# The last 256-column product of row 0 goes from VectorE to a ScalarE copy and a GpSimd multiply

## The chip, the cores and the metric

The kernel runs on one core of one Trainium2 chip. The metric is the device time of one execution in microseconds (us). The kernel before takes 296.96 us as the median of three runs (296.96 to 297.09).

The engines are named as the profile names them. PE is TensorE's matmul, PEld its weight load, DVE is VectorE, ACT is ScalarE, POOL is GpSimd, SP is SyncE. A name with a q behind it (POOLq, SPq, ACTq) is the queue of that engine, where semaphore waits, branches, drains and the issue of transfers appear. PSUM is held in eight banks of 128 x 512 float32.

## The reference

```python
batch, m, k, n = 16, 512, 1024, 768
x:  (batch, m, k) float32      w1, w2: (k, n) float32

y1 = np.matmul(x, w1)
y2 = np.matmul(x, w2)
return (np.tanh(y1) * y2).astype(np.float32)
```

Seen as a matrix, x has 8192 rows of 1024, which are 64 row blocks of 128. Each of the two products has 768 columns.

## The kernel before, in words

**Tiling.** The matrices are cast to float16. The columns of both weights are put into three blocks of 512: block a is the first 512 columns of w1, block b the first 512 columns of w2, and block g holds the last 256 columns of w1 and the last 256 columns of w2 side by side. For each row block the output needs the tanh of a times b (512 columns) and the tanh of the left half of g times its right half (256 columns).

**Head.** The first four row blocks (`HEAD`) are computed plainly, 8 matmuls for each of the three blocks, while the weights are still arriving. Their x is brought in on SP, cast by DVE (`cx..`), transposed on PE (`PT..`), and copied out of PSUM by `evacuate` (`e..`) on ACT or DVE. The part of the fourth row block that needs block b is done at the very end as filler (`m3y0..` and `m3y1..`, 8 short matmuls each, then the multiplies `mub3X` and `mub3Y`).

**Triples.** The other 60 row blocks come in 20 triples. A triple (three row blocks, two halves of the 1024, three column blocks) would need 18 products of 4 matmuls each. A bilinear scheme makes it 15 products, `p0` to `p14`, of sums of x blocks (`S..`, on DVE) with sums of weight blocks (`B..`, on DVE, once). The results are put together in PSUM by copies and seeds on ACT (`copy..`, `seed..`) and by additions on DVE (`add..`), as the list `C_OPS` says. Then follow the tanh on ACT (`t0`..`t2` for 512 columns, `th0`..`th2` for 256) and the multiply on DVE (`m0`..`m2` for 512, `mh0`..`mh2` for 256), and the rows are stored from SP, at the end also from ACT.

**A check beside it.** Absolute sums of every x row block (`D..`, 1024 columns on ACT, written to a scratch tile called `junk`) and of the weights (`aw..`) are compared with limits; five small steps (`flag_1` to `flag_5`) make one flag `bad`. After the last step of the plan every engine loads `bad` (L817) and branches (L818, `tc.If`) around `general_path`, which isn't run here. After that comes the end of the program (put down to L911): each engine drains, and they meet at a barrier. In program order these instructions stand behind everything that the plan has put on the same engine.

**The order of the work.** The class `Planner` (L75) makes it before the program is built. Each step is an `op` with a name, its cost on each engine that may do it, a due time and its needs; the planner plays the steps through with these costs, takes for each engine the step that can start first (or is due first), gives out the PSUM banks and returns one list. Every instruction is then pinned in that order (`pin`). So a changed cost can change the order on all engines and the number of the banks, and a step with one engine in its costs is always on that engine. The order of the 15 products on PE is strict (`plan.strict`), as three strings give it (`PE_ORDER`, `FIRST_ORDER`, `LAST_ORDER`).

**Around the change.** Before the plan's list, `constants` (L335) runs the seven matmuls of `WARM` (L250) on a constant tile while nothing has arrived yet; each goes to a PSUM bank of its own. `by_pe` (L587) gives the costs of the transposes and of the copies `e..` behind them: 0.5 on ACT for the first four row blocks and for the next three. POOL has the loads of x with a cast (L362), of block b (L359), and 18 tiny copies that hold the loads back (L501); after the last load at L362 the plan gives it nothing.

At the end, the last five steps on DVE are `add4`, `m1`, `mh1`, `mh0` (all of the last triple) and `mub3Y`; the last ones on ACT are `th1` and `th0`. The last four stores are `st620` (row block 62, columns 0 to 511) on ACT, `st621` (row block 62, columns 512 to 767) on SP, `st611` (row block 61, the 256 columns that `mh0` makes) on ACT, and `st3Y` on SP.

Of the kernel before, what the change touches and what calls it, by code (L numbers as in the profile page):

```python
# [9 lines left out]
ALU = mybir.AluOpType  # L10
# [64 lines left out]
class Planner:  # L75
# [9 lines left out]
    def op(self, name, engines, due, needs, fn, *args, behind=(), issued=(), chains=(), xfer=0.0, latency=None, seeds=False,  # L85
           lands=None, hold=0.0):
        assert name not in self.ops, name
        self.ops[name] = dict(engines=engines, due=due, needs=[n for n in needs if n], behind=[n for n in behind if n], issued=[n for n in issued if n], fn=fn, args=args,
                              chains=chains, xfer=xfer, latency=latency, seeds=seeds, lands=lands, hold=hold)
        for c in chains:  # L90
            self.chains.setdefault(c, {"left": 0, "bank": None, "end": 0.0, "act": 0.0, "dve": 0.0})["left"] += 1
# [135 lines left out]
def kernel(  # L227
# [7 lines left out]
    nc = tc.nc  # L235
# [6 lines left out]
    F = 512  # L242
    G = N - F
    HEAD = 4
    TRIPLES = (MT - HEAD) // 3
# [1 line left out]
    FP32 = ((0, 0), (1, 0))  # L247
    LOW, HIGH = 512.0, 1024.0
    XT_BUFS, XH_BUFS, S_BUFS, O_BUFS, C_BUFS = 12, 8, 2, 9, 2
    WARM = 512, 512, 512, 512, 512, 512, 512  # L250
    FILL = 512, 512, 256
    FREE = 3
    TURNS = (2, 0, 1), (0, 2, 1)
# [6 lines left out]
    bf16, f16, f32, i32 = mybir.dt.bfloat16, mybir.dt.float16, mybir.dt.float32, mybir.dt.int32  # L260
# [17 lines left out]
    junk = once.tile([P, K], f16, name="junk")  # L278
# [29 lines left out]
    pin = tc.keep_in_program_order  # L308
    engine = {"dve": nc.vector, "act": nc.scalar, "pool": nc.gpsimd, "sp": nc.sync}
    plan = Planner(8)  # L310
    op = plan.op

    def bank(chain):
        return banks[plan.chains[chain]["bank"]]
# [108 lines left out]
    def out_tile(mt):  # L423
        return o_bufs[mt if mt < HEAD else HEAD + (mt - HEAD) % O_BUFS]
# [21 lines left out]
    def place(i, name):  # L446
        if name[0] == "c":
            return bank((i, name))
        return c_bufs[name, i % C_BUFS]

    def slot_casts(name):
        n = S_NAMES.index(name) * C_BUFS
        return [f"c{s}{k}" for j, (s, k) in enumerate(slices) if s != "b" and n <= j % SLOTS < n + C_BUFS] + [f"cx{HEAD + 2}0"] * (n <= STAGED < n + C_BUFS)
# [19 lines left out]
    def c_mul(e, i, r, src, lo, n, at):  # L473
        o = out_tile(HEAD + 3 * i + r)[:, lo:lo + n]
        pin(nc.vector.tensor_tensor(o, o, place(i, src)[:, at:at + n], ALU.mult))  # L475

    def c_aside(e, r, src, borrowed):
        pin(nc.scalar.copy(out_tile(borrowed)[:, :F], place(0, src)))

# [77 lines left out]
    for n, what in enumerate(by_pool):  # L557
        if what in GATES:
            after, src = GATES[what]
            op(f"gate{what}", {"pool": 0.1}, 0.1 * n, [after], gate, src, issued=issued)  # L560
            issued = [f"gate{what}"]
        if what[0] == "b":
            name = f"c{what}"
            op(name, {"pool": 0.58}, 0.1 * n, [], load_w, "b", int(what[1]), issued=issued, lands=lands[what])
        else:
            mt, h = int(what[1]), what[2:]
            free = [f"cx{m}{k}" for m in range(2, HEAD) for k in range(2) if xh_place(m) == xh_place(mt)]
            name = f"L{mt}{'abc'[int(h)] if h else ''}"
# [18 lines left out]
    def by_pe(mt, h, due, load):  # L587
        fp32 = (mt, h) in FP32
        op(f"PT{mt}{h}", {"pe": 0.44 if fp32 else 0.24}, due, [load], transpose_pe, mt, h, ("T", mt, h), chains=[("T", mt, h)])
        op(f"e{mt}{h}", {"dve": 0.6 if fp32 else 0.45, "act": 0.5} if mt < HEAD else {"act": 0.5}, due + 0.4, [f"PT{mt}{h}"], evacuate, mt, h, ("T", mt, h),  # L590
           chains=[("T", mt, h)])

    for n, after in enumerate(("PT00", "PT10")):
# [25 lines left out]
    outs = {mt: [] for mt in range(MT)}  # L619

    def reuse_out(mt):
        aside = [f"{name}.0" for name, (borrowed, _) in ASIDE.items() if mt == borrowed]
        return aside + [f"st{mt - O_BUFS}"] if mt >= HEAD + O_BUFS else []
# [16 lines left out]
    for n, s in enumerate("agb"):  # L640
        for mt in range(HEAD):
            if (s, mt) == ("b", HEAD - 1):
                continue
            due, behind = (lambda n: landed[slices["agb".index(s) * KO + n]] + 0.8 + 0.02 * mt), []
            finals(mt, s, due(KO - 1) + (5.0, 3.0, 7.0)["agb".index(s)], plain(mt, s, due, behind))

    mt = HEAD - 1
# [31 lines left out]
    def w_needs(v, ks=slice(0, KH)):  # L679
        if v in wsum:  # L680
            return [f"B{v}.{p.start}" for p in parts(v) if p.start < ks.stop and ks.start < p.stop]
        bit = v.bit_length() - 1
        return [f"c{s}{bit // 3 * KH + k}" for s in "abg"[bit % 3] for k in range(ks.start, ks.stop)]
# [5 lines left out]
    def x_needs(i, v):  # L689
        if v & (v - 1):  # L690
            return [f"S{v}.{i}"]
        bit = v.bit_length() - 1
        mt = HEAD + 3 * i + bit // 2
        return [f"e{mt}{bit % 2}"] if mt < BY_PE else [f"T{mt}"]
# [7 lines left out]
    def needed(i, v):  # L702
        return min([slot_of[i, o[0]] for o in C_OPS if o[1] == "p" and o[4] == v] + [needed(i, u) - 0.5 for u, a, b, _ in A_SUMS if v in (a, b)])

    for i in range(TRIPLES):
        for name, kind, needs, *_ in C_OPS:
            soonest[i, name] = max([until[i, n] for n in needs] + ([slot_of[i, name]] if kind == "p" else []))
            until[i, name] = soonest[i, name] + TIME[kind] + 0.2
        for v, a, b, how in A_SUMS:
            op(f"S{v}.{i}", {"dve": 0.335}, None, x_needs(i, a) + x_needs(i, b), x_sum, i, v, a, b, how,  # L710
               hold=needed(i, v) - S_AHEAD if i > 1 else 0.0,
               behind=[f"{r}.{i - S_BUFS}" for r in a_readers[v]] if i >= S_BUFS else first_done)
            for u in (a, b):
                if not u & (u - 1):
                    xt_readers[HEAD + 3 * i + (u.bit_length() - 1) // 2].append(f"S{v}.{i}")
        for o in C_OPS:
            name, kind, needs = o[:3]
            needs = [f"{n}.{i}" for n in needs]
            chains = sorted({(i, p) for p in o[3:6] if isinstance(p, str) and p[0] == "c"})
            if kind == "p":  # L720
                needs += x_needs(i, o[4]) + w_needs(o[5])
                op(f"{name}.{i}", {"pe": SLOT}, slot_of[i, name], needs, product, i, *o[3:], chains=chains,
                   behind=[f"m{HEAD - 1}y0{KO - 1}"] if (name, i) == ("p3", TRIPLES - 1) else [])
                if not o[4] & (o[4] - 1):
                    xt_readers[HEAD + 3 * i + (o[4].bit_length() - 1) // 2].append(f"{name}.{i}")
                continue
            if kind in ("seed", "copy", "add"):
                before = []
                if o[3][0] == "s":
                    before = [f"{r}.{i - C_BUFS}" for r in readers[o[3]]] if i >= C_BUFS else slot_casts(o[3])  # L730
                if kind == "add":
                    op(f"{name}.{i}", {"dve": 0.6}, None, needs, c_add, i, *o[3:], behind=before, chains=chains, seeds=True)
                else:
                    op(f"{name}.{i}", {"act": 0.495}, None, needs, c_copy, i, *o[3:], behind=before, chains=chains, seeds=True)
                continue
            r = o[3]
            mt = HEAD + 3 * i + r
            due = soonest[i, name] + LAST
            if kind in ("t", "th"):
                lo, n = (0, F) if kind == "t" else (F, G)  # L740
                op(f"{name}.{i}", {"act": 0.5 if n == F else 0.285}, due, needs, c_tanh, i, r, o[4], lo, n, o[5],
                   behind=reuse_out(mt) + ([f"{FIRST_READER[name]}.{i}"] if i == TRIPLES - 1 and name in FIRST_READER else []), chains=chains)
            elif i == 0 and name in ASIDE:
                borrowed, at = ASIDE[name]
                op(f"y{name}.0", {"act": 0.5}, due + 1, [n for n in needs if n[0] != "t"], c_aside, r, o[4], borrowed, chains=chains)
                op(f"{name}.0", {"dve": 0.6}, at + 6, [f"y{name}.0"] + [n for n in needs if n[0] == "t"], aside_mul, r, borrowed, hold=at)
                outs[mt].insert(0, f"{name}.0")
            elif kind == "m" and i < HALVED:
                for t in range(2):
                    op(f"{name}{'xy'[t]}.{i}", {"dve": 0.335}, due + 1, needs, c_mul, i, r, o[4], t * G, G, t * G, chains=chains)  # L750
                    outs[mt].append(f"{name}{'xy'[t]}.{i}")
            else:
                lo, n, at = (0, F, 0) if kind == "m" else (F, G, G)
                op(f"{name}.{i}", {"dve": 0.6 if n == F else 0.335}, due + 1, needs, c_mul, i, r, o[4], lo, n, at, chains=chains)
                outs[mt].insert(0 if kind == "m" else 1, f"{name}.{i}")
    for mt in range(MT):
        i = (mt - HEAD) // 3 if mt >= HEAD else -1
# [29 lines left out]
    for mt in range(HEAD, MT):  # L787
        i, r = divmod(mt - HEAD, 3)
        r = turn[mt] - HEAD - 3 * i
# [13 lines left out]
    pin(nc.vector.memset(ones, 2.0 ** -12))  # L803
    for n, cols in enumerate(WARM):
        constants(banks[n], cols)
    for n in sorted(soon, key=lambda n: plan.start_of[n]):
        o = plan.ops[n]
# [3 lines left out]
    for n in order:  # L811
        if n not in soon:
            o = plan.ops[n]
# [102 lines left out]
```

## Time and profile before

| | |
|---|---|
| median of three runs | 296.96 us |
| the profiled execution | 297.16 us |
| its span, from the first to the last instruction | 295.6 us (1.56 us less) |
| mean granted TensorE clock | 1.000 |
| PE busy | 289.5 us, 98% of the span, 1374 matmuls |
| DVE busy | 255.8 us, 87%, 552 instructions |
| ACT busy | 224.4 us, 76%, 454 instructions |
| POOL busy | 42.3 us, 14%, 94 instructions |

Times in the views are counted from the start of the span. A row of the timeline has the start, the length, the engine, the line, the operation, what it writes and reads, how many instructions it merges, and in brackets the idle time before them with what ended it. In a view of one line, three numbers with strokes are the shortest, median and longest duration in ns, then follow the start of the first and of the last in us. Instructions of the queues (POOLq and so on) aren't counted as busy.

### The profile page before, as it was taken

To read this page: it belongs to the slowest core of one execution; us is meant where nothing else is said; L and a number is where in the kernel's file an instruction comes from. 1 tells how busy PE (TensorE), PEld (TensorE's weight loads), DVE (VectorE), ACT (ScalarE), POOL (GpSimd) and SP (SyncE) were. 2 spreads that over 40 slices of the span, in tenths; PEclk is the share of its full clock that TensorE was granted. 3 is DMA by queue.
4 is the path that set the end of the run, shared out by engine and by line. 5 is a ranking of instruction groups with operands and counts; after the bars stand their busy time and mean duration, and the time that the engine had idled before them with its cause. 6 is when DMAs were issued, how large, how long until landed. Compare 5 with 4: busy or idle time off the path is not lost. (4 is left out here: it accounts for less than half of the span.)

```text
span 295.6 us, 4588 instructions
## 1 busy us (share of the span) xinstructions
PE 289.5 (98%) x1374; PEld 132.3 (45%) x1374; DVE 255.8 (87%) x552; ACT 224.4 (76%) x454; POOL 42.3 (14%) x94
## 2 busy tenths in 40 slices
PE   7999999999999999999999999999999999999994
PEld 3445444444444444444444444444444444444442
DVE  1679999999989998898989888898988889898875
ACT  2698599799878878877888888677777767778442
POOL 0065022202102102202012021020211100000000
PEclk9999999999999999999999999999999999999999
DMA  6999999999999999989999999999999999241234
GB/s 217 391 321 204 182 141 169 210 247 230 240 194 197 247 226 216 252 218 239 204 190 246 231 236 270 164 271 264 224 298 225 213 175 324 104 162 53 109 136 169
DMA packets 84858, 63.63 MB, mean 215 GB/s; under 512 B 62816, under 2 KB 67168, under 8 KB 84832
## 3 DMA queue, kind: packets, MB, share of 16 engines
q1 hardware_dynamic: 73888, 45.10, 59.7%
q0 software_dynamic: 9936, 16.65, 36.0%
q10 hardware_dynamic: 1008, 1.57, 1.5%
q8 instruction: 11, 0.18, 0.2%
q14 instruction: 15, 0.12, 0.1%
HBM read 39.85 MB, written 25.17 MB: 220 GB/s over the span
## 5 line engine op out<-in xcount | busy, mean ns | idle before, releaser
L457 PE MATMUL bank<-b,early_x 128*128 128x512 f16 x640 | 148.3, 379 | 0.0
L457 PEld LDWEIGHTS <-early_x 128*128 128x128 f16 x800 | 78.1, 98 | 94.3 <-DVE early_x L421 0.3
L467 DVE TENSOR_TENSOR bank<-bank,arena 128x512 f32<-128x512 f32 x100 | 69.6, 696 | 13.6 <-ACT arena L461 10.9
L461 ACT ACTIVATE arena<-bank 128x512 f32<-128x512 f32 x100 | 57.6, 596 | 18.1 <-PE bank L457 18.1
L475 DVE TENSOR_TENSOR o<-o,bank 128x256 f32<-128x256 f32 (+1 forms) x128 | 61.9, 516 | 7.3 <-ACT o L470 5.9
L390 ACT ACTIVATE junk<-xh 128x1024 f16<-128x1024 f16 x60 | 63.4, 1057 | 0.1
L457 PEld LDWEIGHTS <-xT 128*128 128x128 f16 x400 | 39.0, 98 | 46.9 <-issue 0.4
L457 PE MATMUL bank<-b,xT 128*128 128x512 f16 x240 | 58.3, 379 | 0.0
L470 ACT ACTIVATE o<-bank 128x256 f32<-128x256 f32 (+1 forms) x80 | 34.8, 438 | 26.0 <-DVE bank L467 22.8
L457 PE MATMUL bank<-wh,xT 128*128 128x512 f16 x160 | 41.0, 379 | 0.0
L457 PE MATMUL bank<-wh,early_x 128*128 128x512 f16 x160 | 40.9, 379 | 0.0
L362 POOL DMA_DIRECT2D xh<-in_x_dram x61 | 32.4, 540 | 16.6 <-ACT junk L390 8.6
L421 DVE TENSOR_TENSOR early_x<-early_x,xT 128x512 f16<-128x512 f16 x80 | 33.5, 420 | 0.5
L470 ACT ACTIVATE o<-arena 128x512 f32<-128x512 f32 x40 | 25.2, 629 | 7.5 <-DVE arena L467 7.5
L501 POOL CAST held<-xT 128x1 f32<-128x1 f16 x18 | 4.5, 251 | 161.3 <-DMA xT<-xh 161.3
L461 ACT ACTIVATE bank<-bank 128x512 f32<-128x512 f32 x40 | 21.4, 570 | 4.7 <-PE bank L457 3.9
L430 PE MATMUL bank<-wh,xT 128*128 128x512 f16 x72 | 19.5, 379 | 0.3
L467 DVE TENSOR_TENSOR arena<-bank,arena 128x512 f32<-128x512 f32 x20 | 13.7, 686 | 3.6 <-ACT arena L461 3.6
L421 DVE TENSOR_TENSOR early_x<-xT,xT 128x512 f16<-128x512 f16 x40 | 16.7, 418 | 0.0
L421 DVE TENSOR_TENSOR early_x<-xT,early_x 128x512 f16<-128x512 f16 x40 | 16.7, 418 | 0.0
L467 DVE TENSOR_TENSOR bank<-arena,bank 128x512 f32<-128x512 f32 x20 | 13.8, 692 | 0.1
L390 ACT ACTIVATE junk<-wh 128x768 f16<-128x768 f16 x16 | 13.6, 847 | 0.1
(51 smaller groups left out, 140.0 us busy)
## 6 DMA issues: line engine op xcount, KB each, us to landing
out_dram<-o SPq DMA_DIRECT2D x59, 384.0 KB, 5.1
xh<-in_x_dram POOLq DMA_DIRECT2D x58, 256.0 KB, 6.7
arena<-in_w_dram SPq DMA_DIRECT2D x12, 256.0 KB, 5.6
early_x<-in_x_dram SPq DMA_DIRECT2D x8, 256.0 KB, 4.9
arena<-in_w_dram ACTq DMA_DIRECT2D x4, 256.0 KB, 5.9
wh<-in_w_dram POOLq DMA_DIRECT2D x8, 128.0 KB, 5.5
xT<-xh SPq DMA_TRANSPOSE x57, 4.2
out_dram<-o SPq DMA_DIRECT2D x3, 256.0 KB, 2.5
```

Of the source, the lines that this page charges most:

```text
L362: pin(nc.gpsimd.dma_start(xh(mt)[:, cols], xf[mt][:, cols]))
L390: pin(nc.scalar.activation(junk[:, :src.shape[-1]], src, ACT.Abs, scale=scale, accum_out=sums[:, column:column + 1]))
L421: pin(engine[e].tensor_tensor(x_operand(i, v), x_operand(i, a), x_operand(i, b), OP[how]))
L430: pin(nc.tensor.matmul(bank(chain)[:, :rhs.shape[-1]], xt(mt)[:, k, :], rhs, start=first, stop=k == KO - 1, skip_group_check=True))
L457: pin(nc.tensor.matmul(place(i, dst), x_operand(i, a)[:, k, :], w_rhs(b, k), start=begins and k == 0, stop=k == KH - 1, skip_group_check=T ...
L461: pin(nc.scalar.activation(place(i, dst), place(i, src), ACT.Copy, scale=float(sign)))
L467: pin(nc.vector.tensor_tensor(place(i, dst), a, b, ALU.add if signs == (1, 1) else ALU.subtract))
L470: pin(nc.scalar.activation(out_tile(HEAD + 3 * i + r)[:, lo:lo + n], place(i, src)[:, :n], ACT.Tanh, scale=float(sign)))
L475: pin(nc.vector.tensor_tensor(o, o, place(i, src)[:, at:at + n], ALU.mult))
L501: pin(nc.gpsimd.tensor_copy(held, xt(mt)[:, 0, :1]))
```

## The change

Three things are changed. `WARM` has its last matmul of 512 columns cut into two of 256, the second of which goes to the eighth bank. The planner's cost of a copy `e..` on ACT is 0.59 in place of 0.5 for the first four row blocks. And in the last triple `mh0` isn't done by DVE out of PSUM: a new step `ymh0` lets ACT copy the 256 columns from PSUM to the scratch tile `junk`, and `mh0` multiplies them into the output tile on POOL. It can only be on POOL, at a cost of 0.7 in the plan.

The order that follows from it: on DVE the last steps are `add4`, `m1`, `mh1`, `mub3Y`. On ACT `ymh0` stands behind `th0`, ahead of the stores. The last stores are `st620` and `st3Y` on SP, `st621` and `st611` on ACT. On POOL the multiply stands behind the last load of x and ahead of POOL's load of `bad` and its branch. In the head, the copy `e31` goes from DVE to ACT, the abs pass `D1` moves from before the first weight casts to behind them, `D2` and `D3` each move one place back (`D3` now stands between `e61` and `e40`), and `p10` of the first triple comes ahead of `PT51`. Some steps of ACT and DVE in the first four triples change places, and on SP the store `st4` comes ahead of the transpose `T16`. From there to the end the order on every engine is the same as before, with other bank numbers.

```diff
-    WARM = 512, 512, 512, 512, 512, 512, 512
+    WARM = 512, 512, 512, 512, 512, 512, 256, 256
...
+    def c_spare(e, i, src, at):
+        pin(nc.scalar.copy(junk.bitcast(f32)[:, :G], place(i, src)[:, at:at + G]))
+
+    def spare_mul(e, r):
+        o = out_tile(HEAD + 3 * (TRIPLES - 1) + r)[:, F:F + G]
+        pin(nc.gpsimd.tensor_tensor(o, o, junk.bitcast(f32)[:, :G], ALU.mult))
...
-        op(f"e{mt}{h}", {"dve": 0.6 if fp32 else 0.45, "act": 0.5} if mt < HEAD else {"act": 0.5}, ...
+        op(f"e{mt}{h}", {"dve": 0.6 if fp32 else 0.45, "act": 0.59} if mt < HEAD else {"act": 0.5}, ...
...
+            elif (name, i) == ("mh0", TRIPLES - 1):
+                op("ymh0", {"act": 0.29}, due + 0.3, needs[:1], c_spare, i, o[4], G, chains=chains)
+                op(f"{name}.{i}", {"pool": 0.7}, due + 1, ["ymh0"] + needs[1:], spare_mul, r)
+                outs[mt].insert(1, f"{name}.{i}")
```

More of the change, by code (lines that the diff above doesn't have):

```diff
@@ L589, in by_pe @@
         op(f"PT{mt}{h}", {"pe": 0.44 if fp32 else 0.24}, due, [load], transpose_pe, mt, h, ("T", mt, h), chains=[("T", mt, h)])
-        op(f"e{mt}{h}", {"dve": 0.6 if fp32 else 0.45, "act": 0.5} if mt < HEAD else {"act": 0.5}, due + 0.4, [f"PT{mt}{h}"], evacuate, mt, h, ("T", mt, h),
+        op(f"e{mt}{h}", {"dve": 0.6 if fp32 else 0.45, "act": 0.59} if mt < HEAD else {"act": 0.5}, due + 0.4, [f"PT{mt}{h}"], evacuate, mt, h, ("T", mt, h),
            chains=[("T", mt, h)])
```

## The prediction

> **What bounds the kernel now.** I read the busy times by stage first, from 60 us on and then the end.
>
> ```profile
> core 0: us, PE busy (x) PEld busy (x) DVE busy (x) ACT busy (x) POOL busy (x), PEclk, DMA share, GB/s
> 60.00:100.00 40.00, 40.00 (x187) 18.11 (x186) 37.65 (x87) 35.12 (x74) 5.36 (x12) 1.00 1.12 224
> 250.00:280.00 30.00, 30.00 (x142) 13.62 (x140) 25.74 (x58) 21.21 (x42) 0.00 (x0) 1.00 0.31 122
> 290.00:295.60 5.60, 1.33 (x11) 0.78 (x8) 2.04 (x5) 0.66 (x2) 0.00 (x0) 1.00 0.59 209
> ```
>
> PE is busy in all of both middle stages, at a granted clock of 1.00. The change takes no matmul away, so the middle cannot get shorter; it could only get longer if PE were made to wait. What is left to gain or lose lies in the head and in the last stage, where PE has 1.33 us of work in 5.6. The groups of PE by shape show how little PE idles:
>
> ```profile
> L457 PE MATMUL bank<-b,early_x 128*128 128x512 f16 x640 | 148.3, 379 | 0.0
> L430 PE MATMUL bank<-wh,xT 128*128 128x512 f16 x72 | 19.5, 379 | 0.3
> L337 PE MATMUL bank<-ones 128*128 128x512 bf16 x11 | 4.4, 538 | 1.3 <-DVE ones L803 1.3
> ```
>
> The end is read from the timeline, DVE, ACT and the two queues that store:
>
> ```profile
> 289.66 0.69 DVE L467 TENSOR_TENSOR bank<-arena,bank 128x512 f32<-128x512 f32 x1
> 290.29 1.04 PE L430 MATMUL bank<-wh,xT_kept 128*128 128x256 f16 x8
> 290.39 0.66 ACT L470 ACTIVATE o<-bank 128x256 f32<-128x256 f32 x2 [1.06 <-DVE bank L467]
> 290.55 1.35 DVE L475 TENSOR_TENSOR o<-o,bank 128x512 f32<-128x512 f32 x3 [0.19 <-issue]
> 291.27 1.17 ACTq L427 DMA_DIRECT2D out_dram<-o  x2
> 291.81 0.41 DVE L437 TENSOR_TENSOR o<-o,bank 128x256 f32<-128x256 f32 x1
> 292.26 0.33 SPq L427 DMA_DIRECT2D out_dram<-o  x1
> ```
>
> The DVE row of three is `m1`, `mh1`, `mh0`; the row at 291.81 is `mub3Y`, which ends at 292.22. SP then issues the last store at 292.26. The queue of SP waits for it, and the program ends after a barrier:
>
> ```profile
> SPq L911 <- DMA out_dram<-o: 0.8, 3, 0.3
> L911 SPq DRAIN  x3: 7/7/130, 294.7 to 295.3; - x3
> L911 POOLq EVENT_SEMAPHORE  x4: 17/17/17, 294.7 to 295.5; - x4
> ```
>
> SP's first drain stands at 294.7, when the stores have landed. POOL's first wait at the barrier is met at 294.7 too, and 0.9 us later the span is over. So today the last store sets the end, and POOL is ready early. How early, and with what, is the row on which this prediction rests. POOL's queue, from its load of `bad` on (lines 817, 818 and 911):
>
> ```profile
> L817 POOLq TENSOR_LOAD <-bad x1: 496/496/496, 274.3 to 274.3; - x1
> L818 POOLq COMPARE_BRANCH  x2: 38/42/45, 274.9 to 276.8; - x2
> L818 POOLq INC_SWDGE_SEM  x1: 1576/1576/1576, 275.2 to 275.2; - x1
> L911 POOLq DRAIN  x3: 45/107/5758, 277.2 to 295.3; - x3
> L911 POOLq DRAIN  x2: 45/76/107, 294.9 to 295.3; - x2
> ```
>
> The last line is the same view from 290 us on: the two late drains took 45 and 107 ns, so the one of 5758 ns is the one that began at 277.2. From the load of `bad` at 274.3 POOL needs 0.5 for the load, 1.6 for the semaphore step, a branch, and 5.76 for the drain, until 277.2 + 5.76 = 283.0: 8.6 us. Today nobody sees them, since they are over 11.7 us before the barrier.
>
> **The change part by part.**
>
> *The copy of 256 columns on ACT.* `th1` and `th0` are the ACT row at 290.39: two in 0.66, each 0.38, so the second starts 0.28 behind the first and ends at 291.05. `ymh0` reads the same bank and follows at the same step: start 290.95, and at the 0.38 of a 256-column ACT row it ends at 291.33. ACT's stores begin at 291.27 only, so the copy delays the first one of ACT at most to 291.33, and that one is now `st621`, which needs `mh1` (the DVE row of three ends at 291.90, and `mh1` one step of 0.33 before, at 291.57). Cost on the path: nothing.
>
> *DVE without `mh0`.* `mub3Y` moves up by one step of 0.33 (from 291.81 to 291.48; PE's last matmul has ended by 290.29 + 1.04 = 291.33). Its store on SP moves to 291.93.
>
> *The multiply on POOL.* The trace has no two-input operation on POOL. The nearest rows:
>
> ```profile
> 1.26 0.29 POOL masks.py:199 TENSOR_SCALAR_AFFINE_SELECT ident<-ident 128x128 f32<-128x128 f32 x1
> L475 DVE TENSOR_TENSOR o<-o,bank 128x256 f32<-128x256 f32 x80 | 31.9, 416 | 5.2 <-ACT o L470 5.2
> 17.68 0.44 POOL L504 CAST held<-wh 128x1 f32<-128x1 f16 x1 [16.13 <-DVE wh L368]
> 17.18 0.43 DVE L368 CAST wh<-arena 128x512 f16<-128x512 f32 x1 [0.78 <-DMA arena<-in_w_dram]
> ```
>
> Twice the 0.29 of 128 columns is 0.58; twice DVE's own 0.42 is 0.83. Lower end 0.42, upper end four times DVE, 1.7; I take 0.7, near the POOL row with room for the second input. The start: the cast at 17.68 began 0.07 after the DVE row it waited for ended (17.61). So the multiply runs from 291.40 to 292.10, and `st611` can be issued on ACT at 292.13, against 292.26 for the last issue today. By the data alone, then, the end comes 0.13 us earlier; with the multiply at 0.83 it is even, at 1.7 it is 0.9 later, and at 0.42 the bound is `st3Y`, 0.33 earlier. In a sentence beside it: the Trainium skill, GPSIMD Engine Reference, section 3.1, gives about 2.6 cycles of 1.2 GHz for an element of such an operation, an estimate of 0.55 us for 256 and a dispatch on top; the sum by it stays the same within 0.1.
>
> *What is queued behind the multiply.* This decides. Until now POOL went from its last load of x straight to its load of `bad`, at 274.3. Now the multiply stands ahead of it, and POOL's sequencer gets past it only when ACT's copy is done, at 291.40. DVE's row shows that a sequencer then runs on while its engine works:
>
> ```profile
> L817 DVEq TENSOR_LOAD <-bad x1: 539/539/539, 291.4 to 291.4; - x1
> ```
>
> (291.4, before DVE's last multiply starts at 291.81.) So POOL loads `bad` at 291.4 and not at 274.3, and the same 8.6 us of load, semaphore step, branch and drain end at 300.0. If the load has to wait for the multiply to be done (292.1), it is 300.7. The barrier, met at 294.7 so far, is met at 300.0 to 300.7; the 0.9 behind it stays. I take 300.0, because of the DVE row. The stores have landed by 294.6 and no longer matter. The span grows by 300.0 - 294.7 = 5.3.
>
> For the drain: bounds are 0 (it waited for something that would be over by then) and 5.76. I take 5.76. Nothing on POOL was running but its own semaphore step, its last transfer had been issued at 236.8, and its waits of line 911 begin at 294.7 only:
>
> ```profile
> 236.81 0.53 POOL L362 DMA_DIRECT2D xh<-in_x_dram  x1 [2.87 <-ACT junk L390]
> ```
>
> The Trainium skill, Perfetto Trace Analysis, section "Sequencer-only Instruction (DRAIN, etc)", says that such a row holds execution only and not the wait for a semaphore; with that, the 5.76 would be POOL's own work.
>
> *The copies at 0.59 in the plan.* They change the head's order. PE up to `PT01` is as before. Then two places matter. `e31` on ACT ends as early as on DVE, and the g block's first matmul waits for the weight cast at 17.18 + 0.43 in any case. And `D3` now runs between `e61` and `e40`:
>
> ```profile
> 25.10 1.05 ACT L390 ACTIVATE junk<-early_x 128x1024 f16<-128x1024 f32 x1
> 26.55 0.59 ACT L366 COPY xT<-bank 128x512 f16<-128x512 f16 x1 [0.31 <-PE bank L380]
> 27.68 1.07 ACT L366 COPY xT<-bank 128x512 f16<-128x512 f16 x2 [0.54 <-PE bank L380]
> 28.79 0.43 DVE L421 TENSOR_TENSOR early_x<-xT 128x512 f16<-128x512 f16 x1
> 31.40 1.89 PE L457 MATMUL bank<-b,early_x 128*128 128x512 f16 x8
> ```
>
> `e61` starts at 26.55, the next step on ACT 0.49 later, `D3` takes 1.05, so `e40` starts at 28.1 in place of 27.68 and ends at 28.7, just when PE, with `p10` moved ahead, comes to `PT51`, which goes into the same bank. The first sum `S3` needs `e41` and starts at 29.2 in place of 28.79; but `add64` (0.6) now comes after `S15`, so `S15`, for which `p6` (at 31.40) waits, ends at about 31.0 in place of 31.3. PE loses nothing here; bounds -0.1 and +0.4, and I take 0. The moved steps of the first triples have the slack of the row 60 to 100, where DVE idles 2.3 us of 40 and PE does not: 0.
>
> *The warm-up cut in two.* One more weight load and matmul while PE waits:
>
> ```profile
> 1.30 3.17 PE L337 MATMUL bank<-ones 128*128 128x512 bf16 x7 [1.30 <-DVE ones L803]
> 4.67 0.44 PE L380 MATMUL bank<-ident,early_x 128*128 128x128 f32 x1 [0.21 <-DMA early_x<-in_x_dram]
> ```
>
> The seven end at 4.47 and the first transpose waits for x until 4.67: hidden; 0.15 at most.
>
> **The sum.** Span 295.6 + 5.3 = 300.9; outside the span there are 1.56, so 302.5 for the profiled execution, which was 0.20 above the median. Predicted for the median: 302.3 us.
>
> **The rivals.**
>
> *The drain is short when it comes late.* For it: at the start a drain of POOL took 184 ns, and behind a semaphore step of 27 ns:
>
> ```profile
> L900 POOLq INC_SWDGE_SEM  x1: 27/27/27, 0.1 to 0.1; - x1
> L900 POOLq DRAIN  x1: 184/184/184, 0.6 to 0.6; - x1
> ```
>
> Then POOL is ready at 291.4 + 8.6 - 5.76 = 294.3, just ahead of the stores, and the end is that by the data: 0.13 earlier, 296.85 us, no change. It decides when the drain takes under 0.4 us. The Trainium skill has a rule that says this: VectorE: DVE Perf Modes, section "The DRAIN you can't avoid", puts such drains of the program's frame at a constant 12 ns or so on all five engines. SP's 7 ns agree with that; POOL's 5758 do not, and the measurement decides. Chance 0.22.
>
> *The multiply itself is slow when first used.* The semaphore step, done at the end, cost 1.58 and 5.76 for what followed; if the multiply costs 5.8, POOL's semaphore step begins at 297.2 and the drain ends 7.8 later (275.2 to 283.0), at 305.0: 307.3 us. Against it: affine select took 0.29 on its first use, and the first cast 0.44 against 0.25 in the mean. It counts from about 0.8 us of multiply on, which the load of `bad` and the branch cover. Chance 0.06.
>
> *Something of the drain only*, half of it: 299.4. Chance 0.04.
>
> *Faster by over 0.2%.* 0.33 at the end and 0.3 from the head's idle (the 0.3 in the second PE row) together would be 0.6: 296.3. Chance 0.03.
>
> **How the numbers follow.** The forecast (own range 301.3 to 303.6: the load of `bad` waits or not, the multiply from 0.42 to 1.7, the head +-0.3) has 0.65. Slower has 0.65 + 0.06 + 0.04 = 0.75; same 0.22; faster 0.03. A measurement of this kernel can tell about 0.2%, 0.6 us, from no change. Without the first rival only 0.75 would be held, so the range reaches down to it: 296.7 to 303.6.
>
> **What the profile after would show.** POOL's load of `bad` at 291.4 or 292.1; its drain at about 294.3, some 5.76 long; the other engines waiting at the barrier to 300. `st611` issued at 292.1 and landed by 294.5. PE's last matmul at 291.3 +-0.3. The prediction is wrong if that drain is under a microsecond, or if PE idles anew in the head.

## The result: 1.6% slower, and the profile after

The changed kernel takes 302.34 us (median of 5 runs, 302.22 to 302.61), the kernel before 297.09 (296.96 to 297.96, 5 runs of the same comparison). The ratio is 1.0163, 95% interval 1.0130 to 1.0196. Ratios here and below leave out executions that lie over 1.5% above the fastest of their kernel, and they aren't the ratios of the medians. The forecast was 302.3.

The middle is as before: between 40 and 280 us PE is busy all the time in both kernels. The page of the changed kernel, its second part (40 slices of 7.5 us) and its fourth (the chain that ended last):

```profile
PE   7999999999999999999999999999999999999970
...
POOL 0065032202202022022022022020220200000000
PEclk9999999999999999999999999999999999999995
...
PE bank L457 86%; PE bank L430 5%; DMA arena<-in_w_dram 4%; ACTq L357 0%; PE bank L380 0%; DVE o L475 0%; DVE wh L368 0%; SPq L347 0%; SPq L357 0%; POOLq L828 0%; POOL o L482 0%; PE bank L502 0%
```

The last slice is empty for PE; in the kernel before it was not (PE had 1.33 us in the last 5.6). PE's granted clock, 0.9 or more in every other slice, reads 0.5 in this one, in which PE has no work. The chain goes through POOL's load of `bad` (L828) and the multiply (L482). The timeline of the changed kernel from 290.3 us on, in the columns of the prediction:

```profile
290.38 1.04 PE L430 MATMUL bank<-wh,xT_kept 128*128 128x256 f16 x8
290.48 0.66 ACT L470 ACTIVATE o<-bank 128x256 f32<-128x256 f32 x2 [1.07 <-DVE bank L467]
290.64 1.02 DVE L475 TENSOR_TENSOR o<-o,bank 128x512 f32<-128x512 f32 x2 [0.19 <-issue]
291.03 0.38 ACT L478 COPY junk<-bank 128x256 f32<-128x256 f32 x1
291.49 0.72 POOL L482 TENSOR_TENSOR o<-o,junk 128x256 f32<-128x256 f32 x1 [54.06 <-ACT junk L478]
291.58 0.42 DVE L437 TENSOR_TENSOR o<-o,bank 128x256 f32<-128x256 f32 x1
291.69 0.89 ACTq L427 DMA_DIRECT2D out_dram<-o  x2
```

This is the last work on data: the last store is issued by 292.58 (291.69 + 0.89). The span goes on to 301.0. What fills the 8.4 us is in the views of three lines of the changed kernel, its load of `bad` (L828), its branch (L829) and the end of the program (L922):

```profile
L828 POOLq TENSOR_LOAD <-bad x1: 498/498/498, 291.4 to 291.4; - x1
...
L829 POOLq INC_SWDGE_SEM  x1: 1576/1576/1576, 292.3 to 292.3; - x1
...
L922 POOLq EVENT_SEMAPHORE  x4: 17/17/17, 300.1 to 300.9; - x4
L922 POOLq DRAIN  x3: 45/107/5755, 294.3 to 300.6; - x3
L922 SPq DRAIN  x3: 7/7/130, 294.8 to 300.6; - x3
...
L922 ACTq EVENT_SEMAPHORE  x2: 17/17/17, 300.2 to 300.9; - x2
```

POOL loads `bad` at 291.4, spends 1.58 us in its semaphore step, and begins the drain of 5.76 us at 294.3. SP is ready at 294.8, when all stores have landed. POOL comes to the barrier at 300.1, and ACT, which has been idle for 6 us, gets past it at 300.2. The three steps are as long as before; they only begin 17.1 us later (291.4 against 274.3), and 5.4 us of that stick out (barrier met at 300.1, before at 294.7).

### The profile page after: what moved, and what is told of

Read it like the earlier page. It is cut to its first block, busy times and chain, and to the rows that moved or that the text cites. A ratio compares the mean times of both kernels' runs of the same rounds, so it can differ in the third digit from the quotient of the medians.

```text
span 301.0 us, 4588 instructions
## 1 busy us (share of the span) xinstructions
PE 289.2 (96%) x1375; PEld 131.9 (44%) x1375; DVE 255.1 (85%) x550; ACT 224.9 (75%) x456; POOL 42.9 (14%) x95
## 3 DMA queue, kind: packets, MB, share of 16 engines
q0 software_dynamic: 9936, 16.65, 35.8%
## 4 chain that ended last, share of the span: by engine, by line
PE 91%; DMA 4%; DVE 0%; ACTq 0%; SPq 0%; issue 0%; POOLq 0%; POOL 0%
PE bank L457 86%; PE bank L430 5%; DMA arena<-in_w_dram 4%; ACTq L357 0%; PE bank L380 0%; DVE o L475 0%; DVE wh L368 0%; SPq L347 0%; SPq L357 0%; POOLq L828 0%; POOL o L482 0%; PE bank L502 0%
```

## The experiments

The theory: POOL's end of program (load of `bad`, semaphore step, drain: 8.6 us) stands in program order behind POOL's last piece of work, and the late multiply drags it past the end of the data. Its rivals: the multiply or its data cost the time; the copy and the new order of the head cost it; or the drain is short by itself and only waits for something. After these runs a second question came up: what makes the drain so long.

### One part of the change at a time

The first run takes only `mh0` back to DVE and leaves the warm-up cut and the plan's 0.59:

```diff
-            elif (name, i) == ("mh0", TRIPLES - 1):
-                op("ymh0", {"act": 0.29}, ...)
-                op(f"{name}.{i}", {"pool": 0.7}, due + 1, ["ymh0"] + needs[1:], spare_mul, r)
-                outs[mt].insert(1, f"{name}.{i}")
```

> The changed kernel with the last 256-column product put back on VectorE; the two warm-up matmuls of 256 and the planner's 0.59 stay. Theory (POOL's end work stands behind a late multiply): the 5.3 us are gone, 297.0 us, within 0.4 of the kernel before; POOL's load of the flag is back at 274.3 and its long drain at 277.2. Rival (the new order of the head costs time): it stays above 298 us, with new idle time of PE between 10 and 35 us.

The second is the kernel before with these four lines and the two helpers they call, and nothing else:

> The kernel before with only the copy on ScalarE and the multiply on GpSimd; warm-up and the planner's cost as before. Theory: 302.3 us, the whole loss, with a POOL drain of 5.76 us from about 294.3 on. Rival (head): 297.0 us.

Measured: 297.49 us (297.05 to 300.54, 10 runs) for the first, ratio 1.0016 (0.9992 to 1.0041); 302.42 (302.37 to 302.58, 4 runs) for the second, ratio 1.0172 (1.0155 to 1.0189); the kernel before beside them took 297.10. POOL's load and drain in the first kernel:

```profile
L824 POOLq TENSOR_LOAD <-bad x1: 497/497/497, 274.2 to 274.2; - x1
...
L918 POOLq DRAIN  x3: 45/107/5758, 277.1 to 295.6; - x3
```

and in the second:

```profile
L828 POOLq TENSOR_LOAD <-bad x1: 492/492/492, 291.4 to 291.4; - x1
...
L922 POOLq DRAIN  x3: 45/107/5756, 294.3 to 300.6; - x3
```

The step with ACT and POOL carries the whole loss; the plan's cost and the split warm-up cost nothing that can be measured.

### The multiply or its place

Here `mh0` is back on DVE, out of PSUM; ACT's copy stays, and all that POOL does with it is to copy one column:

```diff
-                op(f"{name}.{i}", {"pool": 0.7}, due + 1, ["ymh0"] + needs[1:], spare_mul, r)
+                op("touch", {"pool": 0.1}, due + 1, ["ymh0"], gate, junk.bitcast(f32)[:, :1])
+                op(f"{name}.{i}", {"dve": 0.335}, due + 1, needs, c_mul, i, r, o[4], F, G, G, chains=chains)
```

> The changed kernel with the multiply on VectorE out of PSUM again; the copy on ScalarE stays, and in place of the multiply GpSimd copies a single column of it to its own scratch value, which nobody waits for. Theory: POOL still comes to its load of the flag at 291.4 only, so 302.3 us although nothing waits for POOL's work and its work is 0.2 us. Rival (the multiply itself is dear, by its length or by what it does to the last store): 297.0 us.

302.46 us (302.40 to 302.58), ratio 1.0175 (1.0158 to 1.0192): as slow as the change, with no data of the output on POOL at all. The views of its copy, load and end of program:

```profile
L511 POOL COPY held<-junk 128x1 f32<-128x1 f32 x1 | 0.2, 183 | 54.1 <-ACT junk L478 54.1
```

```profile
L829 POOLq TENSOR_LOAD <-bad x1: 493/493/493, 291.3 to 291.3; - x1
...
L923 POOLq DRAIN  x3: 45/107/5760, 294.1 to 300.5; - x3
```

0.18 us of work in place of 0.72 (the first row is of the grouped lines: busy us, mean ns), and the same drain at the same time. What costs is where POOL's last instruction stands, and not how long it takes.

### The semaphore step

The branch skips `general_path`, in which four transfers are issued from POOL (two of weights, one of x, one of the result). In this run they are issued from SP, so that the branch skips no transfer of POOL:

```diff
-            nc.gpsimd.dma_start(wf[t], wr[t])
+            nc.sync.dma_start(wf[t], wr[t])
```

(and the same for `xt32` and `o`; `general_path` isn't run in either kernel). The two theories here were that the drain is the tail of the semaphore step, and that it is work of its own.

> The changed kernel with the four transfers of the general path, which is not run, issued by SyncE in place of GpSimd. POOL then has no semaphore step at the branch. Theory A (the long drain is the end of what the semaphore step began): the drain is under 0.3 us, POOL is ready at 292.6, the stores set the end again: 297.0 us. Theory B (the long drain is a cost of its own of a POOL that has issued transfers): the drain of 5.76 us begins 1.6 to 1.9 us sooner, at 292.5, and ends at 298.2: 300.4 us.

300.51 us (300.42 to 300.62), ratio 1.0110 (1.0093 to 1.0127). No semaphore step is in the trace any more, and the drain has kept its length:

```profile
L828 POOLq TENSOR_LOAD <-bad x1: 494/494/494, 291.0 to 291.0; - x1
...
L922 POOLq EVENT_SEMAPHORE  x4: 17/17/17, 297.8 to 298.5; - x4
L922 POOLq DRAIN  x3: 45/107/5754, 292.0 to 298.4; - x3
```

So the drain is not the tail of that step. From the load of `bad` to the barrier it is 6.8 us (291.0 to 297.8) in place of 8.6: 1.8 less, of which the step is 1.58, and the time is 1.83 less.

### A drain ahead of time

One drain is added to the changed kernel, right behind POOL's last load of x, where POOL then has 54 us of nothing to do:

```diff
+            if n == f"L{loads[-1]}":
+                drain_pool()
```

(`drain_pool` is a helper with the one statement `pin(nc.gpsimd.drain())`.)

> The changed kernel with one drain of GpSimd put into the order right behind its last load of x, at about 237, long before the multiply. Theory B1 (the long drain at the end clears up behind the transfers that POOL has issued, once): the early one is long and hidden, the one at the end under 0.5 us, POOL is ready at 294.0 to 294.4 and the stores set the end: 297.0 us. Theory B2 (every such drain costs 5.76 us, or the first thing POOL does after a pause is dear): 302.4 us as before.

297.31 us (297.01 to 301.35, 10 runs), ratio 1.0007 (0.9972 to 1.0041): the loss is gone, with the copy on ACT and the multiply on POOL still there. The added drain (L514) and the end of POOL's queue:

```profile
L514 POOLq DRAIN  x1: 12122/12122/12122, 237.1 to 237.1; - x1
```

```profile
L834 POOLq INC_SWDGE_SEM  x1: 190/190/190, 292.5 to 292.5; - x1
...
L927 POOLq EVENT_SEMAPHORE  x4: 17/17/17, 295.2 to 296.0; - x4
L927 POOLq DRAIN  x3: 39/101/107, 293.2 to 295.8; - x3
```

The end drain is down from 5755 to about 100 ns, and the semaphore step from 1576 to 190. So the length of both depends on what POOL has done since its last drain.

With the early drain and the transfers of `general_path` on SP together:

> The changed kernel with both: the early drain and the transfers of the general path on SyncE. Theory B1: POOL is ready at about 292.6, two microseconds ahead of the stores: 297.0 us, within 0.3 of the kernel before, since the store behind the multiply is issued at 292.25 and the last store of the kernel before at 292.26. Theory B2: 300.5 us.

297.42 us (297.27 to 298.95, 12 runs), ratio 0.9995 (0.9966 to 1.0023). The added drain and those of the end:

```profile
L514 POOLq DRAIN  x1: 10200/10200/10200, 236.4 to 236.4; - x1
...
L927 POOLq DRAIN  x3: 39/99/107, 292.1 to 295.3; - x3
```

POOL is done at 292.2 and the barrier is met at 294.8, when the stores have landed. There is no gain on the kernel before, because there too the end was set by the stores and not by POOL.

### What the drain counts

The drain was put half-way, behind the step `H34`, when POOL had issued 39 of its 69 transfers, first in a single execution, then in ten:

> The changed kernel with one drain of GpSimd in the middle of its loads, behind the hold at about 137, after some 39 of its 69 transfers. Theory B1, with a length that goes by the number of transfers since the last drain: the drain at the end takes about 30/69 of 5.76, 2.5 us, and the time is 299.2 us (or that plus what the loads behind the middle drain come too late). Theory B1 with a length that does not go by their number: 302.4 us. Theory B2: 302.4 us.

> The half-way drain again, timed. If both steps are counted by the transfers that GpSimd has issued since its last drain (39 before the drain, 30 after it), semaphore step 0.80 us and end drain 2.56 us as in the one look, so the end comes (1.576 - 0.796) + (5.755 - 2.563) = 3.97 us ahead of the changed kernel: 298.4 (+-0.3). If the one look was an accident of that execution: anything else between 297.1 and 302.3.

298.68 us in the single one; 298.53 (298.25 to 300.78) in the ten, ratio 1.0042 (1.0017 to 1.0067). The rows of the profiled execution of the ten, the half-way drain first:

```profile
L514 POOLq DRAIN  x1: 3467/3467/3467, 124.7 to 124.7; - x1
...
L834 POOLq INC_SWDGE_SEM  x1: 796/796/796, 291.9 to 291.9; - x1
...
L927 POOLq DRAIN  x3: 51/107/2563, 293.2 to 296.3; - x3
```

Then more transfers instead of fewer: the changed kernel with 20 more loads behind the last one, of 16 values in one partition each, and of 16 values in all 128 partitions each:

```diff
+                for j in range(20):
+                    pin(nc.gpsimd.dma_start(spare20[:1, 16 * j:16 * j + 16], xf[0][:1, 16 * j:16 * j + 16]))
```

> The changed kernel with 20 more GpSimd-issued loads behind the last load of x, each of 16 values in one partition. Counted by transfers (82 ns of drain and 20 ns of semaphore step each, from the runs with 69, 30 and 0 open transfers): semaphore step 1.98 us, end drain 7.40 us, time 302.3 + 2.0 = 304.3. Counted by descriptors or bytes, of which these have next to none: both steps as in the changed kernel to a few per cent (1.6 and 5.8 to 6.0 us), 302.3 to 302.6.

> The same 20 loads over all 128 partitions (as many descriptors each as a load of x, 4 KB each in place of 256 KB). By transfers or by descriptors: semaphore step 1.98 us, end drain 7.40 us, 304.3. By bytes: 1.6 and 5.8 us, 302.4.

Their two steps, with one partition:

```profile
L833 POOLq INC_SWDGE_SEM  x1: 1974/1974/1974, 294.3 to 294.3; - x1
...
L926 POOLq DRAIN  x3: 51/107/7324, 296.5 to 304.4; - x3
```

and with 128:

```profile
L833 POOLq INC_SWDGE_SEM  x1: 1969/1969/1969, 293.4 to 293.4; - x1
...
L926 POOLq DRAIN  x3: 45/107/7329, 295.5 to 303.4; - x3
```

Together with the runs above:

| transfers issued by POOL since its last drain | semaphore step, ns | end drain, ns |
|---|---|---|
| 0 (early drain) | 190 | 101 |
| 30 (half-way drain) | 796 | 2563 |
| 69 (the change) | 1576 | 5755 |
| 89 (20 tiny ones more) | 1974 | 7324 |
| 89 (20 of 128 partitions more) | 1969 | 7329 |

From row to row that is 82, 82 and 78 ns of drain and 20 ns of semaphore step for each transfer, whether it moves 128 or 256 KB, as POOL's loads of weights and of x do, or 16 values. What counts is the number of transfers, not the bytes and not the partitions. Nor is it the DMA packets: POOL's queue has 9936 of them in the changed kernel, 144 for each of its 69 transfers, and in the two runs with 20 more 10576 and 12816, which is 32 and 144 for each added one, with the same two lengths.

The times, 306.21 and 305.30 us (one run each), are above the forecast 304.3. In the one-partition run PE waited 2.0 us in the middle of the program, once, on ACT, and everything after it is that much later:

```profile
PE bank L458 <- ACT bank L462: 2.0, 1, 2.0
```

The other run has the same wait with 0.95 us. 304.3 and these waits make 306.3 and 305.25, so they account for both differences. The waits end at 165.0 and 164.0 us, and the first of the 20 loads is issued at 239.5 and 238.5, so the running of these loads can't have caused them; why these two executions have them isn't shown. The two lengths don't depend on it.

### How late POOL's last work may be

A one-column POOL copy was added to the kernel before, first gated on the last ScalarE copy of the last triple (`copy60`), then on `copy63`, two such copies before it:

```diff
+    def touch(e):
+        pin(nc.gpsimd.tensor_copy(held, place(TRIPLES - 1, "s60")[:, :1]))
...
+    op("touch", {"pool": 0.1}, 1e3, [f"copy60.{TRIPLES - 1}"], touch)
```

> The kernel before, with one copy of a single column put on GpSimd that waits for the ScalarE copy which ends at 287.17; nobody waits for it, and the multiply stays on VectorE. Theory (POOL's end work is a fixed 8.6 us behind the last thing that POOL waits for): load of the flag at 287.2, POOL ready at 295.8 in place of 294.75 at the barrier: 1.1 us longer, 298.1 us; a third point on the line through 274.3 (no cost) and 291.4 (5.4). Rival (POOL's work is dear only beside the last stores): 297.0 us.

> The kernel before with one one-column GpSimd copy added, now gated on the next-to-last ScalarE copy of the last triple (it ends at 283.9 in the profiled execution of before), where the run before it was gated on the last one (287.17). In the disturbed execution of that run the GpSimd queue was through its barrier wait 8.94 us after the start of the one-column copy (290.99 to 299.93), so the queue should be done at about 284.0 + 8.9 = 292.9, ahead of the 294.75 at which the barrier was met before. The theory that only the place of GpSimd's last work counts, with a slack of 294.75 - 8.9 = 285.8: no change, 297.1 (+-0.3), end drain 5.76 us starting near 287.1. A rival, that any late GpSimd instruction or a busy GpSimd in the last 10 us costs by itself: 298 or more, as at 287.17.

The later one: median 299.76 us of ten runs that spread widely (298.47 to 304.83; the four lowest lie between 298.47 and 298.78; the kernel before took 297.27 beside it), ratio 1.0056 (1.0028 to 1.0084). That is slower, but the size is badly known: by the interval it lies between 0.8 and 2.5 us, and what spreads the runs isn't shown. The forecast, 298.1, lies below all ten. The profiled execution (302.41 us) was one with a wait of PE of 3.3 us on the transpose of an x block, so that all its times at the end are later; POOL against SP can still be compared within it. The view of waits, then the views of the copy and of the program's end:

```profile
PE bank L457 <- DMA xT<-xh: 3.3, 1, 3.3
```

```profile
L507 POOL COPY held<-arena x1: 183/183/183, 291.0 to 291.0; 128x1 f32<-128x1 f32 x1
...
L915 POOLq EVENT_SEMAPHORE  x4: 17/17/17, 299.9 to 300.7; - x4
...
L915 SPq DRAIN  x3: 7/7/130, 298.4 to 300.4; - x3
```

SP is ready at 298.4, POOL at 299.9, 8.9 us after its copy began. POOL is the last by 1.5 us. The 8.9 are 0.3 more than the 8.6 of the forecast, because the load of `bad` took 0.75 us here. In an execution without the wait of PE the copy would start at 287.2 (the ScalarE copy ahead of it ends at 287.17 in the kernel before), and 287.2 + 8.9 = 296.1 is 1.4 us behind 294.7, an estimate that fits the four lowest runs.

The earlier one: 297.23 us (296.97 to 300.69, 10 runs), ratio 1.0030 (0.9993 to 1.0068), and its profiled span is 295.5. Its copy, drain and barrier:

```profile
L507 POOL COPY held<-arena x1: 183/183/183, 283.1 to 283.1; 128x1 f32<-128x1 f32 x1
...
L915 POOLq EVENT_SEMAPHORE  x4: 17/17/17, 294.7 to 295.4; - x4
L915 POOLq DRAIN  x3: 45/107/5759, 286.2 to 295.2; - x3
```

The copy began 0.9 us sooner than forecast, because the ScalarE copy that it waits for isn't the next-to-last, which the forecast took it for. The drain of 5.76 us ends at 292.0, again 8.9 us after the copy began, and the barrier is met at 294.7 as in the kernel before. GpSimd work that begins 7.4 us before SP is ready (291.0 against 298.4) costs; work that begins 11.6 us before the barrier (283.1 against 294.7) costs nothing that these runs show. The bound by the 8.9 us would be 294.7 - 8.9 = 285.8; no run lies right at it.

## Why the prediction was right

**What bounds.** The middle was unchanged, as said, and the end moved from the stores to POOL's queue, as said.

**The copy on ACT.** Forecast 290.95 to 291.33, measured 291.03 to 291.41. It cost the path nothing.

**The multiply.** Taken at 0.7 us from a POOL row of another kind; measured 0.725, started at 291.49 in place of 291.40. The upper end of 1.7 was too careful. The estimate beside it from the Trainium skill (GPSIMD Engine Reference, section 3.1), 0.55 us and a dispatch, agrees with the 0.725: it leaves 0.17 for the dispatch, and a copy of one column took 0.183.

**The data's end.** Forecast 0.13 us earlier; it came 0.1 later (SP's drain at 294.8 against 294.7). PE's last matmuls begin 0.09 later (290.38 against 290.29) and the multiply took 0.03 more. This small term was wrong in sign, and it lies off the path, since POOL ends 5.3 us behind it. With the drain moved ahead of time it would be what decides, and there the kernel is not measurably different from before (1.0007, 0.9972 to 1.0041).

**POOL's queue.** This was the step on which the forecast rested, and it held in each part. The load of `bad` ran ahead of the multiply (291.4 against 291.49; forecast 291.4, with 292.1 as the other end). Semaphore step 1.576 us, drain 5.755 at 294.3 (forecast 5.76 at 294.3). Barrier 300.1 (forecast 300.0), span 301.0 (forecast 300.9), 302.34 us (forecast 302.3).

**The head and the warm-up.** Taken at 0; the run with these parts alone has 1.0016 (0.9992 to 1.0041). In the profiled execution of the change PE did idle anew in the head, 0.31 us at 8.6 us for a cast of weights, which the prediction had named as a sign of being wrong. The same wait is in the profiles of the two kernels with a one-column copy (0.27 and 0.20), which have the uncut warm-up and the cost of 0.5, so it isn't put down to the change.

**The range.** Its ends don't follow from the parts it names: the upper one comes to 304.3 (a load of `bad` that waits for a multiply of 1.7 us, and 0.3 of the head), where it says 303.6, and the lower one to 302.0 (no such wait), where it says 301.3. Without the first rival it would have held 0.69 (0.65 and 0.04) and not 0.75, since 307.3 lies above it. And 0.13 us off the median of 296.96 is 296.83, not 296.85. None of this touches the forecast.

**The rivals.** *The drain is short when it comes late* fell: it is 5.75 to 5.76 us at 277, 286, 292 and 294 us. What it depends on is POOL's transfers since its last drain; the drain at the program's start, which the rival was built on, has none before it, and its 184 ns fit that. The rule cited for it (the Trainium skill, VectorE: DVE Perf Modes, section "The DRAIN you can't avoid", some 12 ns on all five engines) holds here for SP's first drain (7 ns) and not for POOL's. *The multiply is slow when first used* fell with the 0.725 us. *Half of the drain only* was not seen in this kernel; it can be made, with a drain half-way. The prediction had the length right by taking it from the trace, without knowing what sets it; it carried over because the change leaves the number of POOL's transfers at 69.

## What to carry to other kernels

Before work is given to an idle engine near the end, read what stands behind it in that engine's queue, above all at the end of the program; on GpSimd here that was a load, a semaphore step and a drain, 8.6 us behind 69 transfers, the same behind 0.18 and 0.72 us of work. Where GpSimd has issued as many transfers, give it its last work some 9 us before the end, or let it drain right after its last transfer, where nobody waits. An engine that is 14% busy and idle for the last 54 us isn't free there if its end of program is still to come.

## What the runs showed that was not expected

- The drain of GpSimd at the end costs about 80 ns, and the semaphore step at the skipped branch about 20 ns, for each transfer that GpSimd has issued since its last drain, with little left at 0 transfers (101 and 190 ns; 184 and 27 at the program's start). 16 values count like 256 KB.
- Where a drain comes makes a difference to its own length: half-way, with 39 transfers, it took 3.5 us (89 ns each), but right behind the last load of x 12.1 us, more than the 5.76 that 69 transfers come to at the end. The last loads had not landed yet, and the traces of the two runs with the early drain bear on that: in the first the last load landed at 246.4 (237.2 + 9.2) and the drain of 12.1 us ended at 249.3, in the second it landed at 243.7 (236.4 + 7.3) and the drain of 10.2 us ended at 246.6. Both drains end 2.9 us after the landing, and they differ in length by as much as the landings do. So these drains seem to have waited for transfers still on their way, and such a row isn't GpSimd's own work alone. At the end of the program all had long landed (by 245.8 in the changed kernel). Why the half-way drain has 89 ns for each transfer and not 82 is open.
- An early drain shortened not only the drain but the semaphore step as well (1576 to 190 ns). The drain doesn't take over the work of the step where the step is left out (5754 ns against 5755). What each of the two does is open.
